# First modulation in four parts, keys and values growing in PSUM across them

## The chip, the cores and the metric

The kernel runs on one core of a Trainium2 chip. The core has five engines with a queue each: TensorE (PE in the profile, with its weight loads as PEld), VectorE (DVE), ScalarE (ACT), GpSimd (POOL) and SyncE (SP), which here issues the loads and stores. Matrix products read SBUF and add up in PSUM, which has eight banks of 512 f32 columns by 128 partitions. The metric is the device time in microseconds (us); lower is better.

## The reference

Two layers of a diffusion backbone over 512 latent tokens and 256 context tokens, width 1024. Layer 0 is windowed grouped-query attention (16 query heads of 64, 4 key and value heads, a sink logit, QK-norm, 2-D rotary positions), layer 1 is bidirectional retention; each is followed by a SwiGLU. Everything is modulated by six vectors made from a condition `c` (or `c_ctx`). What matters here is the beginning of layer 0:

```python
mx = jnp.split(c_act @ ada_w[i] + ada_b[i], 6, axis=-1)
mc = jnp.split(cc_act @ ada_w[i] + ada_b[i], 6, axis=-1)
h_x = modulate(rms_norm(x, norm1_g[i]), mx[0], mx[1])
h_c = modulate(rms_norm(y_ctx, norm1_g[i]), mc[0], mc[1])
...
q_x, k_x, v_x = jnp.split(h_x @ w_qkv, [qd, qd + kvd], axis=-1)
q_x = rope_2d(rms_norm(q_x.reshape(B, S, N_HEADS, HEAD_DIM), q_gain), tables)
k_x = rope_2d(rms_norm(k_x.reshape(B, S, N_KV_HEADS, HEAD_DIM), k_gain), tables)
v_x = v_x.reshape(B, S, N_KV_HEADS, HEAD_DIM)
k_c, v_c = jnp.split(h_c @ w_qkv[:, qd:], 2, axis=-1)
k_c = rms_norm(k_c.reshape(B, L, N_KV_HEADS, HEAD_DIM), k_gain)
```

`modulate(h, shift, scale)` is `h * (1 + scale) + shift`; `mx[0]` and `mx[1]` are the shift and the scale of the first normalization, parts 0 and 1 below.

## The kernel before

Activations lie transposed: the 1024 features are eight tiles `k` of 128 partitions, the tokens are columns (stream `s` = 0 has 512 latents, `s` = 1 has 256 context tokens). Each operand of a projection is kept as a rounded high part and a low part that holds the rest, and a product is three matrix products (`mm3`, L138 to L140: high by high, low by high, high by low). Weights arrive as chunks of 128x1024 f32 through `next_w` (L123 loads, ACT casts the high part at L130, DVE subtracts for the low part at L131) in one stream in a fixed order: two key chunks, two value chunks, queries 0, 1 and so on.

The start of layer 0 runs in this order:

- `ada_unit` (L322) makes 512 columns of one modulation part for both conditions: sixteen products, with a stationary operand of two columns, over four loaded tiles of 512 KB, then `ada_finish` copies the two rows (L306), transposes them (L309) and adds the bias (L313). Four units make parts 0 and 1: units 2 and 0 for feature tiles 0 to 3, then units 3 and 1 for tiles 4 to 7. `fold_gain` (L114) folds the gain into the scale.
- `add_square` (L189 to L192) squares on ACT and adds up on DVE; `rms` (L199) sums over partitions with a matrix of ones on PE; `neg_half_rstd` makes the factor from a logarithm, an exponential and a Newton step (L102, L178 to L180).
- `modulate` does three operations for a feature tile: DVE scales (L211), ACT adds the shift and rounds to the high part (L214), DVE makes the low part (L215). The four feature tiles of a half and stream are traced in a row, latents first, then the context.
- When the features are there, `qk_tile` projects a key chunk for latents and then for the context (L138 to L140 into `pj`), and `head_norm` normalizes it: squares, a block matrix of ones `bd` on PE (L391), the factor, and for latents the rotation (a shuffle on DVE L395, a multiplication on POOL L396, a multiplication and an addition on DVE L397 and L398). Then four copies and differences for a pair of heads write the split keys (L425 to L429).
- Six value tiles of 128 tokens follow, each with 24 products of 256 columns into a bank of `pT` (L442 to L444) and a copy by DVE (L446).
- `make_q(j)` projects a pair of query heads for latents and context, takes the sums of squares per token (L468), rotates (L471 to L474) and splits (L480 to L483). `make_q(0)` and `make_q(1)` come ahead of the attention blocks, the others between them.
- `attend` handles a block of 128 queries of one key head: scores (L534 into `S2`), mask and minimum (L535), exponential (L102), normalization (POOL, L548), transposes on PE (L557), products with the values (L569). Three more modulation units are made between blocks by `ada_unit_late` (L336), which uses four groups of 32 columns of the array with a stationary operand padded to 32 columns.

No part of this start has an order written out: the framework's planner takes the instructions in traced order as priorities and orders each engine by its own estimate of what is ready. A tile with a tag shares a number of buffers; an instruction that needs one waits until the earlier owner's last reader is done.

Of the kernel before, what the change touches and what calls it, by code (L numbers as in the profile page):

```python
# [8 lines left out]
F32 = mybir.dt.float32  # L9
# [16 lines left out]
RH = 4  # L26
# [26 lines left out]
def dit_kernel(ctx, tc, xT, cT, crow, small, consts, masks, tabs0, tabs1, jtab, adaN, adaT, wst, out):  # L53
# [212 lines left out]
    St = ExitStack()  # L266
    st_p = St.enter_context(tc.tile_pool(name="st", bufs=1, reuse_waits="tile"))
    nc.sync.dma_start(cst, consts)
    ccol = cp.tile([P, 8, 2], F32, name="ccol")
    rows_t = cp.tile([P, 512], F32, name="rows")  # L270
    silu(ccol, sm_t[:, C_C:C_C + 16].rearrange("p (k s) -> p k s", s=2))
# [3 lines left out]
    dec = sm_t[:, C_DEC:C_DEC + 8]  # L275
    lg = cp.tile([P, 8], F32, name="lg")
    t1 = cp.tile([P, 8], F32, name="lg_t1")
    t2 = cp.tile([P, 8], F32, name="lg_t2")
    t3 = cp.tile([P, 8], F32, name="lg_t3")
    nc.scalar.activation(t1, dec, AF.Abs)  # L280
    lnexp(t1, t1, AF.Exp, scale=-1.0)
    nc.vector.tensor_scalar(t2, t1, 2.0, None, op0=add)
    nc.vector.reciprocal(t2, t2)
    nc.vector.tensor_tensor(t1, t1, t2, op=mult)
    nc.vector.tensor_tensor(t2, t1, t1, op=mult)
    NTERM = 10
    nc.vector.tensor_scalar(t3, t2, 1.0 / (2 * NTERM + 1), None, op0=mult)
    for k in range(NTERM - 1, 0, -1):
        nc.vector.scalar_tensor_tensor(t3, t3, 1.0 / (2 * k + 1), t2, add, mult)
    nc.vector.scalar_tensor_tensor(t3, t3, 1.0, t1, add, mult)  # L290
    nc.vector.tensor_scalar(t1, dec, 0.0, None, op0=ALU.min)
    nc.vector.scalar_tensor_tensor(lg, t3, -2.0, t1, mult, add)
    dcol = cp.tile([P, 4, RH], F32, name="dcol")
    nc.vector.tensor_scalar(dcol[:, 0, :], lg[:, 0:4], 128.0, None, op0=mult)
    nc.vector.tensor_scalar(dcol[:, 1, :], lg[:, 4:8], 640.0, None, op0=mult)
    nc.vector.tensor_scalar(dcol[:, 2, :], lg[:, 4:8], 384.0, None, op0=mult)
    nc.vector.tensor_scalar(dcol[:, 3, :], lg[:, 4:8], -1.0, None, op0=mult)

    ccol32 = cp.tile([P, 8, 32], F32, name="ccol32")
    nc.gpsimd.memset(ccol32, 0.0)  # L300
    nc.gpsimd.tensor_copy(ccol32[:, :, 0:2], ccol)

    def ada_finish(u, o, m):

        part, d0 = u // 2, u % 2 * 4
        nc.scalar.copy(rows_t[0:m, :], o[0:m, :])  # L306
        t = pO()
        for i in range(4):
            nc.tensor.transpose(t[:, m * i:m * i + m], rows_t[0:m, i * P:(i + 1) * P], ident[0:m, 0:m])  # L309
        tv = t[:, 0:4 * m].rearrange("p (d s) -> p d s", s=m)  # L310
        for s in range(2):
            col = mods[0, s][:, part, d0:d0 + 4]
            nc.vector.tensor_tensor(col, tv[:, :, s], sm_t[:, C_ADAB + 4 * u:C_ADAB + 4 * u + 4], op=add)  # L313

    def ada_unit(u, pool, tag, bufs):

        o = pj()
        for kk in range(4):
            w = T(pool, 1024, tag, bufs)
            nc.sync.dma_start(w, adaN[u, kk])  # L320
            for a in range(2):
                nc.tensor.matmul(o[0:2, :], ccol[:, 2 * kk + a, :], w[:, a * 512:(a + 1) * 512],  # L322
                                 start=kk + a == 0, stop=kk + a == 4)
        ada_finish(u, o, 2)

    def ada_unit_late(u):

        part, d0 = u // 2, u % 2 * 4
# [122 lines left out]
    def make_q(j):  # L451
# [5 lines left out]
        for s in range(2):  # L457
# [6 lines left out]
            if s == 0:  # L464
                tot = pj(12)
# [617 lines left out]
```

## Time and profile before

| | us |
|---|---|
| median of 3 runs | 1861.93 (1860.24 to 1863.08) |
| profiled execution, its time | 1867.23 |
| its span | 1865.4 |
| first key product on PE starts | 40.40 |
| last product of query 1 starts | 112.23 |

Rows of the order of work give the start, the duration, the engine, the line, the operation with output and inputs, and in brackets the idle time before it and what ended it. A PE duration includes the depth of the pipeline, so the pace of a run of products is the distance between starts. A group row gives total busy time, mean duration in ns and the idle time of the engine just before. A row of stretches gives length, busy time (and instructions) of PE, PEld, DVE, ACT and POOL, the granted PE clock, the DMA share and GB/s.

### The profile page before, as it was taken

Reading aid. Unit: us, or ns where it says so; the run is one execution under the profiler, and the core shown is the slowest. Engines: PE = TensorE matmul, PEld = TensorE weight load, DVE = VectorE, ACT = ScalarE, POOL = GpSimd, SP = SyncE. Lnnn points to the kernel's source line nnn. Section 1 sums busy time; section 2 is a strip of 40 time slices with the busy share of each in tenths; the row PEclk is TensorE's granted clock in tenths of the full one; section 3 lists DMA queues with packets and bytes.
Section 4 is the critical chain, followed back from the end, with each engine's and each line's share of the span. In section 5 each row is a group of like instructions: output and inputs, shape, how many; then the busy total and the mean of one; then the engine's idle time right before and its main releaser. Section 6 shows DMA issues by size and latency. Waiting matters only on the chain.

```text
span 1865.4 us, 24307 instructions
## 1 busy us (share of the span) xinstructions
PE 1823.1 (98%) x9787; PEld 1513.8 (81%) x9787; DVE 1036.7 (56%) x1806; ACT 628.5 (34%) x1067; POOL 151.2 (8%) x247
## 2 busy tenths in 40 slices
PE   8899999999999999999999999999999999999999
PEld 2777776778888888888878888888888888888887
DVE  6677786888554545363675543552643664443433
ACT  5556675543221212121252322422322442222221
POOL 0034333410000000000011000010010000000000
PEclk9999999999999999999999999999999999999999
DMA  8110006534332325162521220220321223323232
GB/s 303 60 36 24 13 30 198 197 119 147 102 102 91 114 78 168 53 219 69 170 69 46 68 90 23 91 70 21 102 80 34 68 91 102 97 95 101 92 102 79
DMA packets 50945, 177.97 MB, mean 95 GB/s; under 512 B 5648, under 2 KB 6032, under 8 KB 50576
## 3 DMA queue, kind: packets, MB, share of 16 engines
q1 hardware_dynamic: 50832, 176.41, 29.2%
q8 instruction: 77, 1.26, 0.3%
q14 instruction: 36, 0.29, 0.0%
HBM read 174.29 MB, written 2.10 MB: 95 GB/s over the span
## 4 chain that ended last, share of the span: by engine, by line
PE 84%; DVE 7%; ACT 3%; DMA 2%; issue 2%; POOL 1%; SPq 0%; ACTq 0%; DVEq 0%; POOLq 0%
PE pj L138 9%; PE pj L139 9%; PE pj L140 9%; PE gu L138 9%; PE gu L139 9%; PE gu L140 9%; PE guc L140 2%; PE guc L139 2%; PE guc L138 2%; PE pv L138 2%; PE pv L140 2%; PE pv L139 2%; PE pv L834 2%; PE pv L835 2%; PE pv L833 2%
## 5 line engine op out<-in xcount | busy, mean ns | idle before, releaser
L130 ACT CAST whi<-wraw 128x1024 fp32r<-128x1024 f32 x216 | 226.2, 1047 | 394.5 <-PE pj L140 202.5
L131 DVE TENSOR_TENSOR wlo<-wraw,whi 128x1024 fp32r<-128x1024 f32 x216 | 270.0, 1250 | 155.0 <-ACT whi L130 154.3
L138 PE MATMUL gu<-h,whi 128*128 128x512 f32 (+1 forms) x736 | 280.1, 382 | 3.0 <-DVE res L918 3.0
L139 PE MATMUL gu<-h,wlo 128*128 128x512 f32 (+1 forms) x736 | 279.8, 381 | 0.0
L140 PE MATMUL gu<-h,whi 128*128 128x512 f32 (+1 forms) x736 | 279.6, 381 | 0.0
L138 PE MATMUL pj<-h,whi 128*128 128x512 f32 (+1 forms) x544 | 197.7, 364 | 2.8 <-DVE res L225 2.4
L139 PE MATMUL pj<-h,wlo 128*128 128x512 f32 (+1 forms) x544 | 193.5, 356 | 0.7 <-DVE wlo L131 0.7
L140 PE MATMUL pj<-h,whi 128*128 128x512 f32 (+1 forms) x544 | 192.8, 355 | 0.0
L225 DVE SCALAR_TENSOR_TENSOR res<-pj,mod,res 128x512 f32<-128x512 f32 (+1 forms) x160 | 104.7, 656 | 127.1 <-PE pj L140 127.1
L138 PEld LDWEIGHTS gu<-h,whi 128*128 128x128 f32 x736 | 139.0, 189 | 28.9 <-ACT h L214 3.6
L140 PEld LDWEIGHTS gu<-h,whi 128*128 128x128 f32 x736 | 139.0, 189 | 26.8 <-DVE h L215 0.4
L139 PEld LDWEIGHTS gu<-h,wlo 128*128 128x128 f32 x736 | 138.9, 189 | 25.3
L248 DVE CUSTOM_DVE_ANT_0 junk<-adaw,crow_sb,small_sb 128x1024 bf16<-128x1024 f32 x100 | 134.6, 1346 | 34.8 <-DMA adaw<-in_adaT_dram 33.3
L138 PE MATMUL pj<-ax,whi 128*128 128x512 f32 x352 | 138.2, 393 | 0.0
L139 PE MATMUL pj<-ax,wlo 128*128 128x512 f32 x352 | 137.3, 390 | 0.0
L140 PE MATMUL pj<-ax,whi 128*128 128x512 f32 x352 | 136.9, 389 | 0.0
L107 ACT ACTIVATE hn<-gu 128x512 f32<-128x512 f32 x44 | 26.3, 597 | 285.0 <-PE gu L140 285.0
L138 PEld LDWEIGHTS pj<-h,whi 128*128 128x128 f32 x544 | 105.3, 194 | 17.8 <-DVE res L225 3.3
L139 PEld LDWEIGHTS pj<-h,wlo 128*128 128x128 f32 x544 | 105.3, 194 | 14.0 <-issue 1.5
L140 PEld LDWEIGHTS pj<-h,whi 128*128 128x128 f32 x544 | 105.3, 194 | 12.0
L676 DVE TENSOR_TENSOR hn<-hn,gu 128x512 f32<-128x512 f32 x44 | 30.2, 687 | 134.7 <-ACT hn L107 134.7
L140 PE MATMUL guc<-h,whi 128*128 128x256 f32 x352 | 99.6, 283 | 0.0
(232 smaller groups left out, 3398.4 us busy)
## 6 DMA issues: line engine op xcount, KB each, us to landing
wraw<-in_wst_dram SPq DMA_DIRECT2D x216, 512.0 KB, 3.5
adaw<-in_adaT_dram SPq DMA_DIRECT2D x68, 512.0 KB, 3.7
adan<-in_adaN_dram SPq DMA_DIRECT2D x16, 512.0 KB, 7.8
wraw<-in_adaN_dram SPq DMA_DIRECT2D x12, 512.0 KB, 4.1
res<-in_xT_dram SPq DMA_DIRECT2D x16, 256.0 KB, 6.0
res<-in_cT_dram SPq DMA_DIRECT2D x8, 256.0 KB, 7.1
crow_sb<-in_crow_dram SPq DMA_DIRECT2D x2, 1024.0 KB, 5.0
out_dram<-res SPq DMA_DIRECT2D x8, 256.0 KB, 2.0
```

The costliest lines, as they stand in the source:

```text
L107: ins = nc.scalar.activation(out_, in_, AF.Silu)
L130: nc.scalar.copy(hi, raw)
L131: nc.vector.tensor_tensor(lo, raw, hi, op=sub)
L138: nc.tensor.matmul(o, whi, xhi, start=first, stop=False)
L139: nc.tensor.matmul(o, wlo, xhi, start=False, stop=False)
L140: nc.tensor.matmul(o, whi, xlo, start=False, stop=last)
L225: nc.vector.scalar_tensor_tensor(res[d], o, mods[l, s][:, part, d:d + 1], res[d], mult, add)
L248: after(nc.vector.tensor_tensor_reduce(junk, w, row, 1.0, bias, mult, add, col), behind)
L676: nc.vector.tensor_tensor(t, t, uo, op=mult)
L833: nc.tensor.matmul(vo, hi[:, tok], wk_[0][:, cs], start=k == 0, stop=False)
L834: nc.tensor.matmul(vo, hi[:, tok], wk_[1][:, cs], start=False, stop=False)
L835: nc.tensor.matmul(vo, lo[:, tok], wk_[0][:, cs], start=False, stop=k == KT - 1)
```

## The change

1. *Modulation in quarters.* `adaQ` holds the weights of parts 0 and 1 so that one `ada_quarter` of four loaded tiles makes shift and scale of two feature tiles for both conditions. It uses 32-column groups as the late units do: 32 products of 128 columns, one copy, two transposes, six small DVE operations with the gain folded in. The four units of before go; the three late ones stay (`ada_unit`, with the padded stationary operand `ccol`).
2. *An order written out.* The loads are traced in a fixed sequence: latents, quarter 0, three weight chunks, quarter 1, context, the fourth chunk, quarters 2 and 3, rotary tables, masks. PE, DVE and ACT then follow a written order (`manual_schedule`) in which feature tiles are modulated two at a time (`hidden0`: both scalings, both high parts, then both low parts).
3. *Keys and values grow in PSUM.* `keys(s, q)` and `values(s, q)` add the products of the two feature tiles of quarter `q`. Both latent key chunks, the context keys and three banks with two value tiles each stay open over the whole section: all eight banks with the two of `pT`.
4. *After it*, PE alone has a written order: the remaining latent values, the key sums, the pieces of query 0 (`make_q` now returns four pieces) between them, and the last values. All key rotation is on DVE (`rope_key`), the context's two key chunks are normalized as one 512-column tile, and the values are copied by ACT. The score banks open after these copies.
5. The chain that computes the retention decay (`lg`, `dcol`) moves from the start to just ahead of the attention blocks.

```diff
@@ the modulation of the first normalization
-    def ada_unit(u, pool, tag, bufs):
-
-        o = pj()
-        for kk in range(4):
-            w = T(pool, 1024, tag, bufs)
-            nc.sync.dma_start(w, adaN[u, kk])
-            for a in range(2):
-                nc.tensor.matmul(o[0:2, :], ccol[:, 2 * kk + a, :], w[:, a * 512:(a + 1) * 512],
-                                 start=kk + a == 0, stop=kk + a == 4)
-        ada_finish(u, o, 2)
...
+    def ada_quarter_load(q):
+        w = []
+        for i in range(4):
+            w.append(T(st_p, 1024, "adan", 8))
+            nc.sync.dma_start(w[i], adaQ[q, i // 2, i % 2])
+        return w
+
+    def ada_quarter(q, w):
+
+        o = pT()[:, 0:256]
+        for part in range(2):
+            for k2 in range(4):
+                for j in range(4):
+                    k = 2 * k2 + j // 2
+                    c0 = (k % 4) * 256 + j % 2 * P
+                    nc.tensor.matmul(o[32 * j:32 * j + 32, part * P:(part + 1) * P], ccol[:, k, :],
+                                     w[2 * part + k // 4][:, c0:c0 + P], start=k2 == 0, stop=k2 == 3)
+        rows = T(cp, 256, "rows", 2)
+        nc.scalar.copy(rows, o)
+        t = pT()[:, 0:256]
+        for part in range(2):
+            nc.tensor.transpose(t[:, part * P:(part + 1) * P], rows[:, part * P:(part + 1) * P], ident)
...
+        for s in range(2):
+            col = mods[0, s][:, 0:2, 2 * q:2 * q + 2]
+            nc.vector.tensor_tensor(col, tv[:, s, 0], bias, op=add)
+            nc.vector.tensor_tensor(col, tv[:, s, 1], col, op=add)
+            fold_gain(0, s, 0, 2 * q, 2 * q + 2)
...
-    for c in range(2):
-        if c == 0:
-            for s, res in ((0, xr), (1, cres)):
-                for k in range(KT):
-                    add_square(s, k, res[k], eng=nc.vector, tmp=(t_sq, t_sc)[s])
-                rms(s, bank=pT)
-        else:
-            ada_unit(3, st_p, "adan", 8)
-            ada_unit(1, st_p, "adan", 8)
-        for s, res in ((0, xr), (1, cres)):
-            fold_gain(0, s, 0, 4 * c, 4 * c + 4)
-            for d in range(4 * c, 4 * c + 4):
-                h[s].append(h_tiles(s))
-                modulate(0, s, 0, d, res, h[s][d], tmp=t_st)
...
+    res0 = [load_stream(0), None]
+    wq = [ada_quarter_load(0)]
+    load_w(rp, "wraw", 2)
+    load_w(rp, "wraw", 2)
+    load_w(st_p, "adan", 8)
+    wq.append(ada_quarter_load(1))
+    res0[1] = load_stream(1)
+    load_w(st_p, "adan", 8)
+    wq += [ada_quarter_load(2), ada_quarter_load(3)]
...
+    kvx = [pj(), pj()]
+    kvc = pO()
+    kvv = [T(ps_v, 512, "kvv", 3) for _ in range(3)]
...
+    def hidden0(s, *ks):
+        y, ts = ssq[s], []
+        for k in ks:
+            h[s].append(h_tiles(s))
+            ts.append(T(st_p, 512, "hs", 3)[:, :NTOK[s]])
+            nc.vector.scalar_tensor_tensor(ts[-1], res0[s][k], acol[0, s, 0][:, k:k + 1], y, mult, mult)
+            nc.scalar.activation(h[s][k][0], ts[-1], AF.Identity, bias=mods[0, s][:, 0, k:k + 1])
+        for k, t in zip(ks, ts):
+            nc.vector.scalar_tensor_tensor(h[s][k][1], t, mods[0, s][:, 0, k:k + 1], h[s][k][0], add, sub)
+
+    def keys(s, q):
+        for j in range(2):
+            o = kvx[j] if s == 0 else kvc[:, j * SC:(j + 1) * SC]
+            for k in (2 * q, 2 * q + 1):
+                ws = slice(k * P, (k + 1) * P)
+                (whi, wlo), (xhi, xlo) = wkv[j], h[s][k]
+                for i, (a, b) in enumerate(((whi, xhi), (wlo, xhi), (whi, xlo))):
+                    nc.tensor.matmul(o, a[:, ws], b, start=k + i == 0 and (s == 0 or j == 0),
+                                     stop=k == KT - 1 and i == 2, skip_group_check=s == 1)
...
+    with tc.manual_schedule(engines={mybir.EngineType.PE, mybir.EngineType.DVE, mybir.EngineType.Activation}):
+        stats0(0)
+        split_w(st_p)
+        ada_quarter(0, wq[0])
+        hidden0(0, 0, 1)
+        split_w(st_p)
+        keys(0, 0)
+        split_w(rp)
+        squares0(1)
+        ada_quarter(1, wq[1])
+        hidden0(0, 2, 3)
+        values(0, 0)
+        rms(1, bank=pT)
+        keys(0, 1)
+        ada_quarter(2, wq[2])
+        hidden0(1, 0, 1)
+        hidden0(1, 2, 3)
+        hidden0(0, 4, 5)
+        split_w(rp)
+        values(0, 1)
+        ada_quarter(3, wq[3])
+        hidden0(1, 4, 5)
+        keys(1, 0)
+        keys(1, 1)
+        hidden0(0, 6, 7)
+        keys(0, 2)
+        hidden0(1, 6, 7)
+        values(1, 0)
+        values(1, 1)
+        for i, mt in enumerate(mtmp):
+            nc.vector.tensor_copy(mask[:, 4 * i * P:4 * i * P + mt.shape[1]], mt)
+        keys(1, 2)
+        keys(0, 3)
+        keys(1, 3)
...
-            nc.gpsimd.tensor_tensor(qn, qn, rope0[:, 0:512], op=mult)
...
+    for a, b, o in zip(kn, ksq, (kvx[0], kvc, kvx[1])):
+        nc.scalar.activation(b, o, AF.Square)
+        nc.scalar.activation(a, o, AF.Identity, scale=qk_gain[:, 1:2])
...
+        nc.vector.stream_shuffle(yy, t, swap16)
+        nc.vector.tensor_tensor(t, t, rope0[:, 0:512], op=mult)
+        nc.vector.tensor_tensor(yy, yy, rope0[:, 512:1024], op=mult)
+        nc.vector.tensor_tensor(t, t, yy, op=add)
...
+    with tc.manual_schedule(engines={mybir.EngineType.PE}):
+        values(0, 2)
+        rope_key(kn[0])
+        key_factor(0)
+        q0[0]()
+        key_factor(1)
+        for e in range(2):
+            kx[e] = key_parts(e, kn[0])
+        q0[1]()
+        for e in range(2):
+            k1, k2 = key_parts(e, kn[1])
+            kc[e], kc[2 + e] = ((k1[:, c], k2[:, c]) for c in HALVES)
+        q0[2]()
+        values(0, 3)
+        q0[3]()
+        values(1, 2)
+        values(1, 3)
+    vt = []
+    for t in range(6):
+        v = T(akv, 256, "v", 6)
+        nc.scalar.copy(v, kvv[t // 2][:, t % 2 * 256:t % 2 * 256 + 256])
+        vt.append(v)
+    psS.close()
```

More of the change, by code (lines that the diff above doesn't have):

```diff
@@ L52, in dit_kernel @@
 @with_exitstack
[L53 removed]
+def dit_kernel(ctx, tc, xT, cT, crow, small, consts, masks, tabs0, tabs1, jtab, adaQ, adaN, adaT, wst, out):
     nc = tc.nc
@@ L295, in dit_kernel @@
[L295 to L313, printed above, removed]
```

258 lines of the change are left out of this document (136 added, 122 removed).

## The prediction

> **What bounds the kernel now.** I read the page first, then the busy time by stretches, then the order of work on PE around the start, then the groups and single rows that carry durations. The page:
>
> ```profile
> span 1865.4 us, 24307 instructions
> PE 1823.1 (98%) x9787; PEld 1513.8 (81%) x9787; DVE 1036.7 (56%) x1806; ACT 628.5 (34%) x1067; POOL 151.2 (8%) x247
> ```
>
> PE bounds the span. The change touches the start alone, so I cut that out: busy time before the first key product, from there to the end of the second query projection, and the attention blocks.
>
> ```profile
> 0.00:40.40 40.40, 32.81 (x81) 6.79 (x81) 24.96 (x73) 20.77 (x39) 0.86 (x7) 1.00 0.86 329
> 40.40:112.40 72.00, 62.76 (x377) 54.34 (x376) 48.94 (x92) 37.99 (x71) 7.99 (x8) 0.95 0.21 66
> 112.40:300.00 187.60, 182.30 (x1360) 141.48 (x1360) 148.05 (x467) 122.99 (x295) 74.18 (x166) 1.00 0.14 47
> ```
>
> Columns: length, busy PE, PEld, DVE, ACT, POOL, granted clock, DMA share, GB/s. Attention keeps PE busy 97% and DVE 79%, with little DMA: whatever is saved ahead of it moves it forward whole. In the first 40.4 us PE looks busy, but with this:
>
> ```profile
> L322 PE MATMUL pj<-adan,ccol 128*2 128x512 f32 x64 | 30.3, 626 | 6.7 <-DMA adan<-in_adaN_dram 6.7
> 6.29 9.01 PE L322 MATMUL pj<-adan,ccol 128*2 128x512 f32 x16 [6.29 <-DMA adan<-in_adaN_dram]
> 16.75 7.03 PE L322 MATMUL pj<-adan,ccol 128*2 128x512 f32 x16 [0.38 <-DMA adan<-in_adaN_dram]
> 40.40 0.50 PE L138 MATMUL pj<-h,whi 128*128 128x512 f32 x1
> 99.97 0.87 PE L534 MATMUL S<-k,q 128*128 128x256 f32 x6
> 107.07 0.41 PE L534 MATMUL S<-k,q 128*128 128x256 f32 x2
> 112.23 0.28 PE L140 MATMUL pj<-h,whi 128*128 128x256 f32 x1
> ```
>
> Four modulation units of 7 us with two useful output rows. The first key product starts at 40.40, the last query-1 product ends at about 112.4; less eight score products in between (1.3), **111.1** is the mark to compare with: keys, values, queries 0 and 1 projected.
>
> **The change, walked through.** Its first section fixes the order on PE, DVE and ACT, so it can be followed engine by engine with the durations of before; all times of the new kernel are estimates so worked out. Transfers:
>
> ```profile
> 0.00:4.00 4.00, 0.00 (x0) 0.00 (x0) 0.38 (x4) 2.53 (x3) 0.86 (x7) 1.00 0.47 90
> 4.00:10.00 6.00, 3.71 (x5) 0.63 (x6) 3.26 (x21) 0.68 (x3) 0.00 (x0) 1.00 1.00 403
> 10.00:20.00 10.00, 8.95 (x24) 1.85 (x23) 5.19 (x11) 5.41 (x9) 0.00 (x0) 1.00 1.04 399
> 10.73 0.63 ACT L189 ACTIVATE y<-res 128x512 f32<-128x512 f32 x1 [6.02 <-DMA res<-in_xT_dram]
> ```
>
> 0.36 MB by 4 us, then 0.4 MB a us; the first latent tile, 2.6 MB into the queue, landed at 10.73 where the count reaches it at about 9.6, so a landing lags by some 1.2. New order: constants, latents (2.1 MB), quarter 0 (2.1), three projection weights (1.6), quarter 1, context (1.0), fourth weight, quarters 2 and 3. Landings: latents 10.1, quarter 0 15.4, weights 16.7/18.0/19.3, quarter 1 24.5, context 27.1, quarter 2 33.5, quarter 3 about 40. Eight staging tiles serve these 18 loads, so on SP the last tile of quarter 1 waits for PE's first products, and the context, the fourth weight and all later loads queue behind it; there are 2.9 MB already in flight then, so the queue does not run dry. Compute rows:
>
> ```profile
> 23.71 1.13 PE L199 MATMUL pT<-y,ones_sb 128*128 128x512 f32 x2
> 51.12 1.97 PE L391 MATMUL pj<-sq,const_sb 128*128 128x512 f32 x2 [0.58 <-ACT sq L390]
> 28.73 1.41 DVE L211 SCALAR_TENSOR_TENSOR hs<-res,acol,y 128x512 f32<-128x512 f32 x2
> 43.39 1.41 DVE L215 SCALAR_TENSOR_TENSOR h<-hs,mod,h 128x512 fp32r<-128x512 f32 x2
> 36.28 0.88 DVE L211 SCALAR_TENSOR_TENSOR hs<-res,acol,y 128x256 f32<-128x256 f32 x2
> 42.26 1.22 DVE L131 TENSOR_TENSOR wlo<-wraw,whi 128x1024 fp32r<-128x1024 f32 x1
> 41.04 1.04 ACT L130 CAST whi<-wraw 128x1024 fp32r<-128x1024 f32 x1
> 294.69 0.64 PE L336 MATMUL pj<-wraw,ccol 128*32 128x128 f32 x16
> 295.26 0.44 PE L557 MATMUL pT<-const_sb,pr 128*128 128x128 f32 x2
> 296.02 0.31 PE L341 MATMUL pj<-const_sb,rows 128*128 128x128 f32 x1
> 40.56 0.57 ACT L306 COPY rows<-pj 2x512 f32<-2x512 f32 x1 [1.92 <-PE pj L322]
> 42.12 0.23 DVE L313 TENSOR_TENSOR mod<-pO,small_sb 128x4 f32<-128x4 f32 x2
> ```
>
> A quarter uses the form of the late units: 16 instructions issue in 0.57 us, and a quarter has 64, so 2.3 us of PE, then a copy (at most 0.57), two transposes (0.5), six small DVE operations (1.0). Four quarters take 11 us of PE with their transposes where four units took 30; that is the part removed. From the ones product to the modulating DVE operation takes 5.0 us (23.71 to 28.73); with the product at 1.97, as it is after an idle PE, 5.9.
>
> - Latents squared by 11.5, factor at 17.3. Quarter 0: products end 17.6. Its copy stands on ACT behind the cast of the first weight, which waits for that landing (16.7): 18.2; columns on DVE, behind the weight's 1.22 us, at 20.0.
> - First pair: 1.41 + 1.41 on DVE; its first high part lets PE start keys at **21.5**, against 40.40. Second and third weight follow on DVE to 25.6.
> - The context's squares wait for 27.1 and hold ACT to 27.9; behind them stands quarter 1's copy, whose products end at 28.3 anyway. Its columns at 30.2, pair done 33.1.
> - Quarter 2 stands on PE behind four value tiles, the context's ones product and keys: products 35.9 to 38.2, columns 40.1. DVE then does two context pairs (4 × 0.88) and a latent pair (2.8) to 46.8, and the fourth weight's split to 48.1.
> - Quarter 3's products end at 44.3, but its copy is behind the split on ACT: 47.3, columns 49.1. DVE: context pair 1.8, latent 2.8, context 1.8, masks 0.8: 56.6.
>
> From 47.8, after quarter 3's transposes, I find no PE instruction whose inputs come later than its turn. What is left on PE, by these intervals:
>
> ```profile
> 43.77 0.39 PE L139 MATMUL pj<-h,wlo 128*128 128x512 f32 x1
> 44.00 0.40 PE L140 MATMUL pj<-h,whi 128*128 128x512 f32 x1
> 53.10 0.42 PE L139 MATMUL pj<-h,wlo 128*128 128x256 f32 x1
> 53.32 0.42 PE L140 MATMUL pj<-h,whi 128*128 128x256 f32 x1
> 54.88 0.28 PE L139 MATMUL pj<-h,wlo 128*128 128x256 f32 x1
> 55.00 0.28 PE L140 MATMUL pj<-h,whi 128*128 128x256 f32 x1
> 108.49 1.05 PE L468 MATMUL pj<-const_sb,sq 128*128 128x2 f32 x8 [1.02 <-ACT sq L463]
> ```
>
> A 512-column product takes 0.23, a 256-column one 0.12 (0.21 in a slow stretch). Left: context keys 48 × 0.12 = 5.8; latent keys 24 × 0.23 = 5.6; values 96 × 0.12 = 11.5; two queries 48 × 0.23 + 48 × 0.12 = 17; three key sums 3; query sums 2 × 1.4. In all 45.7, so query 1 ends at **93.5** where before it was 111.1: **-17.6**.
>
> **Additions.** The stretch at half speed at 53 shows that a PE gap (47.8 to 50.0) is followed by about 3.4 us at half clock; PE now waits from 44.3 to 47.8, so I add 1.7. The decay chain, 21 small DVE operations, moves from the idle start to the attention's start:
>
> ```profile
> 5.80 1.77 DVE L289 SCALAR_TENSOR_TENSOR lg_t<-lg_t,lg_t 128x8 f32<-128x8 f32 x9
> 60.55 0.68 DVE L397 TENSOR_TENSOR y<-y,rope 128x512 f32<-128x512 f32 x1
> L396 POOL TENSOR_TENSOR hn<-hn,rope 128x512 f32<-128x512 f32 x2 | 3.4, 1697 | 69.3 <-DVE y L395 69.3
> L428 DVE TENSOR_TENSOR k<-hn,k 64x512 fp32r<-64x512 f32 x4 | 2.8, 688 | 0.5 <-ACT k L426 0.3
> ```
>
> At 0.2 each that is 4 us of DVE, which costs between 0 (PE bounds) and 4 (DVE bounds); I take 1, near the lower end, since DVE stands idle a fifth of the attention. Key rotary on DVE: two multiplications of 0.68 replace two of 1.7 on POOL; shorter per key, covered by the values and query 0 on PE, nothing. The value copies go to ACT and the score banks come free only after them, at about 84; until 93.5 PE has query 1 to do, nothing. Sum: -17.6 + 1.7 + 1.0 = **-15**. The profiled execution took 1867.23 (span 1865.4), 5.3 above the median 1861.93; the same 15 off the median gives **1847**.
>
> [...] The first unit above took 9.01 for 16 products and the second 7.03; the products at 53.10, after the gap, are spaced 0.21 against 0.12 at 54.88, and the granted clock of that whole stretch is 0.95: 3.6 us lost in 72, about 7 us at half speed. So the rows charge a gap with one slow stretch. [...]
>
> **Rivals.**
> 1. *The last quarter waits for a staging tile.* If its last load gets the tile of the fourth weight, it is issued after the split at 48.1 and lands 3.5 later, about 52:
>
> ```profile
> wraw<-in_wst_dram SPq DMA_DIRECT2D x216, 512.0 KB, 3.5
> ```
>
>    Columns at 54.5, everything after +5.4, and another slow stretch 1.7: **1854**. Against it: quarter 2's tiles come free at 36.
> 2. *DVE bounds the new second half.* From 56.6 to 93.5 it has three keys (2 × 2.8 rotary, 3 × 2.1 factors, 12 × 0.69 splits: 20), two queries of 5.5 (weight 1.22, rotary 2.1, splits 2.2) and the decay chain of 4: 35 us in 37. At the 79% that DVE held beside a full PE this takes 44: +7, **1854**. For it: 35 in 37 leaves no room for a wait. Against it: the third key (7.7) is not due until later heads.
> 3. *Half clock through the first section.* PE's work from 21.5 to 62 is 35 us at full clock; all of it at half ends near 91, not 62: +29, **1876**, slower than before. It decides from nine slow stretches (9 × 1.7 us = 15). Against it: the 0.95 of before, with 9 us of idle PE in its 72.
> 4. *The round trips eat it.* Each quarter crosses PE, ACT, PE, DVE in fixed order; the walk has columns at 20.0, 30.2, 40.1, 49.1. If each trip is 3.7 longer, the change does not do what it says and nothing is gained: **1862**. Against it: each handover above is counted with the row of the operation itself and the queue ahead of it.
>
> **Numbers.** Forecast 0.60 (own range 1841 to 1853: without the two additions and with DVE 3 us ahead, or with both doubled and one late pair), rival 1 0.11, rival 2 0.14, rival 3 0.08, rival 4 0.07. Leaving out rival 3 and half of 4 and the forecast's far tail gives 1840 to 1860. A measurement here tells about 0.2% (3.7 us) from no change: faster 0.82, same 0.08, slower 0.10.
>
> **What would show it.** Right: first key product near 21.5, four modulation groups of about 2.5 us on PE, end of query 1 near 94 to 96, attention as before and 15 us earlier. Wrong: PE idle beyond 50 us before quarter 3 (rival 1), PE waiting on DVE between 62 and 100 (2), granted clock under 0.8 from 20 to 60 (3), columns much more than 10 us apart (4), or an attention stage longer than before because its order is planned anew.

## The result and the profile after

| | us | ratio to before (95%) |
|---|---|---|
| before, median of 5 runs beside it | 1861.93 (1860.24 to 1866.28) | |
| after, median of 5 runs | 1853.34 (1851.35 to 1854.41) | 0.9951 (0.9936 to 0.9966) |

The change makes the kernel 8.6 us faster; 15 were forecast. The profiled execution of after took 1854.34. Its page:

```profile
span 1852.5 us, 24666 instructions
PE 1798.5 (97%) x9969; PEld 1517.3 (82%) x9969; DVE 1032.3 (56%) x1808; ACT 629.2 (34%) x1064; POOL 150.1 (8%) x243
```

PE still bounds. It is 24.6 us less busy than in the profile of before that was shown, 20.7 less than in a second one (before_again, below), and only part of that came out as time. PE's order of work in the new section (start, duration, what was waited for):

```profile
12.49 2.04 PE L199 MATMUL pT<-y,ones_sb 128*128 128x512 f32 x2 [12.49 <-DVE lg_t L705]
14.47 3.59 PE L310 MATMUL pT<-adan,ccol 128*32 128x128 f32 x64
18.56 0.44 PE L316 MATMUL pT<-const_sb,rows 128*128 128x128 f32 x2 [0.50 <-ACT rows L313]
21.57 0.80 PE L390 MATMUL pj<-h,whi 128*128 128x512 f32 x1 [2.57 <-ACT h L379]
...
29.34 0.44 PE L316 MATMUL pT<-const_sb,rows 128*128 128x128 f32 x2 [1.44 <-ACT rows L313]
...
35.77 1.95 PE L310 MATMUL pT<-adan,ccol 128*32 128x128 f32 x64
38.22 0.44 PE L316 MATMUL pT<-const_sb,rows 128*128 128x128 f32 x2 [0.49 <-ACT rows L313]
...
41.46 1.96 PE L310 MATMUL pT<-adan,ccol 128*32 128x128 f32 x64
46.50 0.39 PE L401 MATMUL kvv<-whi,h 128*128 128x256 f32 x1 [3.09 <-ACT whi L147]
46.77 0.44 PE L316 MATMUL pT<-const_sb,rows 128*128 128x128 f32 x2
...
91.22 0.28 PE L140 MATMUL pj<-h,whi 128*128 128x256 f32 x1
...
94.25 0.61 PE L521 MATMUL pj<-const_sb,sq 128*128 128x2 f32 x4
```

The four quarters are there, the first key product starts at 21.57, and the longest PE gap behind it is at 43.4 to 46.5. Query 1's last product starts at 91.22, and its last sums of squares end at 94.9.

To see where the gain went, the trace is cut at three marks that both kernels have: the start of query 1's last sum of squares, of the last value product of the attention, and of the first product of the feed-forward. The profiled executions differ among themselves, so a second one of before (before_again) stands beside the one shown earlier. Stretches of before, whose first row runs to the first mark (columns as in the prediction):

```profile
0.00:114.00 114.00, 97.07 (x466) 62.23 (x466) 75.47 (x164) 60.31 (x114) 9.93 (x15) 0.97 0.44 158
114.00:336.10 222.10, 214.61 (x1595) 163.30 (x1594) 166.64 (x531) 142.62 (x344) 84.76 (x194) 0.98 0.20 65
336.10:402.80 66.70, 63.92 (x363) 56.02 (x360) 59.67 (x80) 28.68 (x43) 23.35 (x14) 0.97 0.47 156
```

The same of before_again, and what follows the third mark:

```profile
0.00:111.70 111.70, 96.06 (x465) 61.26 (x466) 74.70 (x164) 60.32 (x114) 9.97 (x15) 0.98 0.45 162
111.70:329.60 217.90, 211.79 (x1595) 161.65 (x1594) 166.82 (x531) 142.60 (x344) 84.98 (x194) 1.00 0.20 66
329.60:396.40 66.80, 64.03 (x364) 56.08 (x361) 59.78 (x80) 28.79 (x43) 22.77 (x14) 0.97 0.47 157
396.40:1858.80 1462.40, 1447.39 (x7372) 1232.26 (x7370) 734.81 (x1033) 397.35 (x568) 33.06 (x25) 1.00 0.30 92
```

And the four of after:

```profile
0.00:94.60 94.60, 72.58 (x641) 61.84 (x642) 68.31 (x154) 54.06 (x100) 4.75 (x9) 0.98 0.51 191
94.60:317.10 222.50, 211.79 (x1599) 163.61 (x1598) 168.49 (x543) 149.33 (x355) 91.67 (x196) 0.99 0.18 58
317.10:389.10 72.00, 65.52 (x365) 57.38 (x362) 60.65 (x80) 27.65 (x42) 20.56 (x14) 0.95 0.47 165
389.10:1852.50 1463.40, 1448.64 (x7372) 1234.42 (x7371) 734.87 (x1033) 398.21 (x569) 33.12 (x25) 1.00 0.30 92
```

- **Front:** 111.7 to 94.6, 17.1 gained (19.4 against the other profile of before).
- **Attention:** PE is busy 211.79 in before_again and 211.79 in after, but the stretch grows from 217.9 to 222.5: PE's idle time, length less busy, goes from 6.1 to 10.7. 4.6 given back. The first profile of before is as long as after (222.1) for another reason: granted clock 0.98, idle 7.5.
- **Stage between attention and feed-forward** (output projection, gated addition, modulation): 66.8 to 72.0, 5.2 given back, though nothing in it was edited. PE's idle time there goes from 2.8 to 6.5; the other 1.5 is longer busy time, at a granted clock of 0.95 against 0.97.
- **The rest:** +1.0.

Sum -6.3 between these two profiles, which bracket with the other pair (-12.9) the -8.6 of the medians.

### The profile page after: what moved, and what is told of

Its sections match the earlier page's. It is cut to its first block, busy times and chain, and to the rows that moved or that the text cites. A ratio compares the mean times of both kernels' runs of the same rounds, so it can differ in the third digit from the quotient of the medians.

```text
span 1852.5 us, 24666 instructions
## 1 busy us (share of the span) xinstructions
PE 1798.5 (97%) x9969; PEld 1517.3 (82%) x9969; DVE 1032.3 (56%) x1808; ACT 629.2 (34%) x1064; POOL 150.1 (8%) x243
## 4 chain that ended last, share of the span: by engine, by line
PE 86%; DVE 6%; ACT 3%; DMA 2%; POOL 2%; issue 2%; SPq 0%; DVEq 0%; ACTq 0%; POOLq 0%
PE pj L138 9%; PE pj L139 9%; PE pj L140 9%; PE gu L138 9%; PE gu L139 9%; PE gu L140 9%; PE guc L140 2%; PE guc L139 2%; PE guc L138 2%; PE pT L635 2%; PE pv L138 2%; PE pv L140 2%; PE pv L139 2%; PE pv L943 2%; PE pv L944 2%; PE pv L942 2%
## 5 line engine op out<-in xcount | busy, mean ns | idle before, releaser
L130 ACT CAST whi<-wraw 128x1024 fp32r<-128x1024 f32 x212 | 222.2, 1048 | 387.8 <-PE pj L140 200.5
L131 DVE TENSOR_TENSOR wlo<-wraw,whi 128x1024 fp32r<-128x1024 f32 x212 | 264.7, 1248 | 153.3 <-ACT whi L130 152.5
L138 PE MATMUL pj<-h,whi 128*128 128x512 f32 (+1 forms) x512 | 185.3, 362 | 6.9 <-DVE res L225 6.1
L139 PE MATMUL pj<-h,wlo 128*128 128x512 f32 (+1 forms) x512 | 182.1, 356 | 1.0 <-DVE wlo L131 1.0
L140 PE MATMUL pj<-h,whi 128*128 128x512 f32 (+1 forms) x512 | 181.9, 356 | 0.0
L225 DVE SCALAR_TENSOR_TENSOR res<-pj,mod,res 128x512 f32<-128x512 f32 (+1 forms) x160 | 104.7, 656 | 128.7 <-PE pj L140 128.6
L248 DVE CUSTOM_DVE_ANT_0 junk<-adaw,crow_sb,small_sb 128x1024 bf16<-128x1024 f32 x100 | 134.9, 1349 | 36.7 <-DMA adaw<-in_adaT_dram 32.9
L138 PEld LDWEIGHTS pj<-h,whi 128*128 128x128 f32 x512 | 98.7, 193 | 21.0 <-DVE res L225 7.2
L139 PEld LDWEIGHTS pj<-h,wlo 128*128 128x128 f32 x512 | 98.6, 193 | 13.0 <-DVE wlo L131 1.4
L140 PEld LDWEIGHTS pj<-h,whi 128*128 128x128 f32 x512 | 98.6, 193 | 12.1 <-issue 0.4
```

The lines of the kernel that those rows point to most:

```text
L130: nc.scalar.copy(hi, raw)
L131: nc.vector.tensor_tensor(lo, raw, hi, op=sub)
L138: nc.tensor.matmul(o, whi, xhi, start=first, stop=False)
L139: nc.tensor.matmul(o, wlo, xhi, start=False, stop=False)
L140: nc.tensor.matmul(o, whi, xlo, start=False, stop=last)
L225: nc.vector.scalar_tensor_tensor(res[d], o, mods[l, s][:, part, d:d + 1], res[d], mult, add)
```

## The experiments

The experiments ran in three groups. The runs of a group share a chip and the runs of before beside them, and the ratios are against those.

### Where the missing gain went: the condition rows

The modulation sums of the middle stage need `crow_sb`, a load of condition rows into a tile of the pool `wo`, which is opened after the attention and takes memory that the attention's tiles held. The SP queue's waits, in before_again:

```profile
SPq L230 <- DVE stat L541: 9.7, 1, 9.7
```

and in after:

```profile
SPq L230 <- PE pO L647: 15.7, 1, 15.7
```

The order of work of after at that place:

```profile
316.25 0.75 DVE L225 SCALAR_TENSOR_TENSOR res<-pj,mod,res 128x512 f32<-128x512 f32 x1
...
317.54 0.33 SPq L230 DMA_DIRECT2D crow_sb<-in_crow_dram  x1
...
323.67 1.28 ACT L107 ACT_TABLE_LOAD   x1 [3.79 <-DMA crow_sb<-in_crow_dram]
...
326.06 1.28 DVE L248 CUSTOM_DVE_ANT_0 junk<-adaw,crow_sb,small_sb 128x1024 bf16<-128x1024 f32 x1 [2.36 <-ACT crow_sb L107]
```

The load now waits for the last value products and is issued 1.3 us after the first gated addition (316.25); in before_again it is issued at 324.11, 4.5 ahead of it (328.65). ACT then idles 3.79 for the landing and DVE 2.36 for ACT. The first modulation sum starts 9.8 after the first gated addition, 7.0 in before_again. The theory was that this late load makes the stage longer; the rival, that the order of the work does. Two runs move the load. **rows_early** (from after) lets query 0's weight tile take the first place in the attention's pool, so that `wo` overlays tiles that come free sooner:

```diff
+    wsel[0] = 2
+    w_q0 = next_w(ap, 1)
...
-    wsel[0] = 2
-    q0 = make_q(0)
+    q0 = make_q(0, w_q0)
```

> The changed kernel with the pool of the attention laid out so that its two weight tiles come first (the split of query 0's weights is traced ahead of the normalized keys); the condition rows of the output projection, which take the same memory once the attention pool is closed, then lie on tiles that are read for the last time by the last query projection. Theory 1 (the 6 us that are lost between the end of the attention and the first FFN group come from these rows: their load waits for the last value product and DVE's modulation sums start late): the load is issued at least 5 us ahead of the first gated addition instead of 1 us behind it, PE's 6 us of idle time in that stage shrink to about 2, and the time is 1847 to 1848. Theory 2 (the loss lies in how the planner orders DVE in that stage, whatever the load does): the load moves and the time stays at 1852 to 1854.

**rows_late** (from before) holds the load behind a value product of the last attention block:

```diff
-        nc.sync.dma_start(cr, crow.broadcast_to([P, 2048]))
+        ins = nc.sync.dma_start(cr, crow.broadcast_to([P, 2048]))
+        if late is not None:
+            tc.add_manual_dep(ins.ins, late.ins.name, run_dep, reason="condition rows behind the attention")
...
-    cr = cond_rows(wo_p)
+    cr = cond_rows(wo_p, last_pv[0])
```

> The kernel before with one added wait: the load of the condition rows of the output projection waits for the first value product of the last attention block of the trace. Theory 1: the stage loses 5 to 6 us, 1867 to 1868. Theory 2: the load is late and the time stays at 1862 within 2.

The two kernels themselves ran again on the same chip:

> The changed kernel once more, on the same chip as the two others. Both theories: 1853 within 2, the end of the attention at 317 within 1.5 us of the span, and the first FFN group's end some 6 us later than the attention's gain would give.

> The kernel before once more, for its trace. If the 12.9 us between the two profiled spans are 8.6 in the medians because the first profiled execution of before was a long one, this span is 1859 to 1863, and the stage that is shorter than in the first trace shows where the difference lay. If the span is 1865 again, a profiled execution is longer than a timed one.

Measured: rows_early 1865.19, ratio 1.0019 (1.0010 to 1.0029); rows_late 1861.06, 0.9996 (0.9988 to 1.0005); changed_again 1854.99, 0.9960 (0.9948 to 0.9972); before_again 1860.62 in one run. In changed_again the front ends at 96.9, the attention takes 223.1 and the stage 70.0: the two losses repeat. The stage and, above it, the attention in rows_early:

```profile
94.90:327.70 232.80, 217.82 (x1598) 167.29 (x1599) 168.83 (x541) 146.83 (x351) 89.57 (x197) 0.98 0.19 60
327.70:396.40 68.70, 64.21 (x365) 56.35 (x362) 60.77 (x80) 27.83 (x42) 20.91 (x14) 0.98 0.45 157
```

The stage in rows_late:

```profile
331.00:397.40 66.40, 62.76 (x363) 54.59 (x360) 59.72 (x80) 28.67 (x43) 23.70 (x14) 1.00 0.53 180
```

In rows_late the load is issued at 331.44, 1.3 us behind the first gated addition (330.10), as in after, and the stage is no longer: 66.4 against 66.8, the kernel the same. The lengths hide a little, because this stage ran at a granted clock of 1.00 and that of before_again at 0.97: PE's idle time is 3.6 instead of 2.8. So the late load alone does not make the stage long; that theory falls as the whole cause. But the run repeats the late load and not the late sums. The first sum starts 7.8 behind the first gated addition, against 7.0 in before_again and 9.8 in after, since ACT loads its table here before the rows land, at 333.80, and in after only behind them, at 323.67:

```profile
333.80 1.28 ACT L107 ACT_TABLE_LOAD   x1
```

rows_early shortens the stage by 1.3 (against changed_again) to 3.3 (against after), which leaves 1.9 of the 3.2 to 5.2 us. This rest goes with the order on DVE. PE's waits for the gated addition in the stage (total, times, longest), in before and in after:

```profile
PE pj L138 <- DVE res L225: 2.4, 2, 2.0
PE pj L138 <- DVE res L225: 6.1, 2, 4.3
```

In rows_early this wait is 4.1. DVE's order of work around the third gated addition (L225) and the third modulation sum (L248), in before_again:

```profile
341.00 0.74 DVE L225 SCALAR_TENSOR_TENSOR res<-pj,mod,res 128x512 f32<-128x512 f32 x1
341.66 2.77 DVE L248 CUSTOM_DVE_ANT_0 junk<-adaw,crow_sb,small_sb 128x1024 bf16<-128x1024 f32 x1
```

and in changed_again:

```profile
333.36 3.42 DVE L248 CUSTOM_DVE_ANT_0 junk<-adaw,crow_sb,small_sb 128x1024 bf16<-128x1024 f32 x1
336.70 0.74 DVE L225 SCALAR_TENSOR_TENSOR res<-pj,mod,res 128x512 f32<-128x512 f32 x1
```

The sum comes first in all nine traces with the change, rows_early among them, and the addition first in all five without it. The third addition starts 12.4 us behind the first in before_again, 13.2 in rows_late, 16.1 in rows_early, 17.5 in changed_again and 18.5 in after. So both the load and DVE's new order delay it, the order more; no run set that order alone.

And rows_early loses the whole gain elsewhere: with a front as early as after's (94.9) its attention takes 232.8 instead of 222.5. Idle PE there is 15.0 (232.80 less 217.82), and the same products keep PE busy 217.82 instead of 211.79 at a granted clock of 0.98 (0.99 in after). Its edit touches no attention instruction. What changed is the order that the planner gave them. Read by the names of output and inputs, PE's products in the attention stand in one sequence in before_again, rows_late and the two runs with other units below, in a second one in after, changed_again and every run from after below but query_last; rows_early and query_last have each a sequence of their own.

### What makes the gain

Four parts of the change, one at a time. The prediction wrote the gain as one walk; the question was whether it comes from the cheaper modulation products, from the projection products that run between them, or from the written order, and whether the gap at 43.4 costs anything.

**units_by_groups** (from before): the four units use the 32-column groups of the late ones; nothing else changes.

```diff
-    def ada_unit(u, pool, tag, bufs):
...
-    def ada_unit_late(u):
+    def ada_unit_late(u, pool=rp, tag="wraw", bufs=2, bank=pj):
...
+            ada_unit_late(3, st_p, "adan", 8, pO)
+            ada_unit_late(1, st_p, "adan", 8, pO)
```

> The kernel before with its four first units in the form of the late ones (four groups of 32 columns, 2.3 us of products instead of 7), nothing else changed. Theory A (the gain of the start comes from projecting the first features while the later ones are still being made, and the PE time of the units hardly counts, since the loads end at 36 us and DVE's modulation at 49): first key product at 35 to 38 instead of 40.2, time 1858 to 1860. Theory B (the 19 us of removed PE time are the gain): first key product near 22 to 25, time near 1846.

**products_after** (from after): all key and value products of the first section stand behind the modulation on PE.

```diff
         split_w(st_p)
-        keys(0, 0)
         split_w(rp)
...
         hidden0(0, 2, 3)
-        values(0, 0)
         rms(1, bank=pT)
-        keys(0, 1)
         ada_quarter(2, wq[2])
...
+        keys(0, 0)
+        values(0, 0)
+        keys(0, 1)
+        values(0, 1)
         keys(1, 0)
```

> The changed kernel with all key and value products of the first section moved behind the last modulated feature in the written order (same products, same order among them, the quarters and the pairs as they are). Theory A: PE has 25 us of products left at about 46 instead of 15, so the section ends near 71 instead of 61, and 9 to 10 us of the gain are gone: 1862 to 1865. Theory B: the products only move within the section, 1854 to 1856.

**planner_order** (from after): the first section's order is left to the planner.

```diff
-    with tc.manual_schedule(engines={mybir.EngineType.PE, mybir.EngineType.DVE, mybir.EngineType.Activation}):
+    if True:
```

> The changed kernel without the written order of its first section: the planner orders PE, DVE and ACT there from the same traced instructions. Theory C (the written order carries part of the gain): the first section ends 3 us or more later than 61 and the time is 1857 or more. Theory D (what counts is only that the products can start early): end of the section within 2 us, time 1852 to 1857, the spread that another order of the attention brings.

**split_later** (from after): the fourth weight is split behind quarter 3's modulation, so that quarter 3's copy does not stand behind it on ACT.

```diff
         hidden0(0, 4, 5)
-        split_w(rp)
         values(0, 1)
         ada_quarter(3, wq[3])
         hidden0(1, 4, 5)
+        split_w(rp)
```

> The changed kernel with the fourth weight split after quarter 3 and the third context pair instead of ahead of quarter 3's copy; its values are not needed before the last two quarters. By the walk of the prediction quarter 3's columns come 1.0 to 1.2 us earlier and PE's gap of 3 us before 46.5 shrinks by as much: 1 us gained at the end of the section, time 1852 to 1854. If PE stands behind the split itself, the gap stays.

Measured: units_by_groups 1866.62, ratio 1.0032 (1.0021 to 1.0044); products_after 1864.96, 1.0019 (1.0007 to 1.0031); planner_order 1857.94, 0.9983 (0.9973 to 0.9992); split_later 1854.08, 0.9964 (0.9948 to 0.9979).

products_after has the same cheap quarters, but PE has nothing beside them until they are done. Its stretches:

```profile
20.00:40.00 20.00, 12.23 (x198) 7.62 (x198) 16.63 (x43) 10.94 (x22) 0.00 (x0) 0.66 1.03 416
40.00:60.00 20.00, 15.59 (x91) 14.09 (x92) 12.34 (x28) 6.35 (x12) 0.00 (x0) 0.83 0.14 54
```

Query 1's mark comes at 105.6, 11.0 later than in after and 8.7 later than in changed_again, and the kernel's whole gain is gone. Part of this is the clock: 0.66 and 0.83 over 40 us, 0.96 in after from 21.57 to 61.00. Stage by stage not all of the front is lost, though: 105.6 is still 6.1 ahead of before_again's 111.7. So the early products carry 8.7 to 11.0 of the 14.8 to 17.1, the rest of the change the other 6.1, and the total has nothing left because the attention (223.8) and the stage (70.9) are as long as with the change. units_by_groups takes the other side. PE's order of work there, and ACT's row for the key weight:

```profile
37.98 0.33 PE L318 MATMUL pO<-const_sb,rows 128*128 128x128 f32 x1 [1.85 <-ACT rows L316]
43.59 0.80 PE L138 MATMUL pj<-h,whi 128*128 128x512 f32 x1 [5.28 <-ACT whi L130]
...
42.51 1.03 ACT L130 CAST whi<-wraw 128x1024 fp32r<-128x1024 f32 x1
```

The units need little PE time, but the first key product comes at 43.59 instead of 40.40: PE waits 5.28 for the cast of the key weight, which ACT does at 42.51, behind three feature tiles of the modulation, and in before at 37.61. So taking PE time off the units alone gains nothing here; ACT's other order and the lower clock (0.90 to the mark) are part of this result. Most of the front's gain is that projection products run in the idle time between the quarters. Whether they would have found that time beside the wide units, with their 30 us of PE, no run shows. The written order is worth some 3 to 4.6 us of the time (planner_order against changed_again 1854.99 and after 1853.34), 1.4 to 3.7 of it at the front, whose mark comes at 98.3. In split_later the gap ahead of quarter 3's transposes is 2.42, waiting for the copy, where after has 3.09, and the time is that of after. The edit shortens the gap by 0.7 us only, so it does not tell what the gap costs.

### The clock, the place of query 0, and the rotary engine

The slower units_by_groups could be explained by the clock alone. **units_groups_warm** adds six products without use to each unit (from units_by_groups), **gaps_filled** ten such products to the new start (from after):

```diff
+        t = bank()
+        if tag == "adan":
+            for _ in range(6):
+                nc.tensor.matmul(t, ones, w[:, 0:512], start=True, stop=True)
+        t = t[:, 0:P]
```

> The kernel before with its first units in column groups, as in units_by_groups, and six products of the ones matrix with a loaded weight tile added to each unit, whose results nobody reads; they give PE back the busy time that the wide units had. Theory E (units_by_groups is 4 to 5 us slower than the kernel before because PE, less busy, runs at half clock for 24 us of the start): the half-clock stretches between 20 and 60 shrink to one of 3.4 us or none, first key product at 40 or earlier, time 1859 to 1862. Theory F (it is slower through another order of DVE and ACT): stretches shrink and the time stays at 1865 to 1867.

```diff
+        t = pT()
+        for _ in range((0, 1, 0, 3)[q]):
+            nc.tensor.matmul(t, ones, res0[0][0], start=True, stop=True)
+        t = t[:, 0:256]
...
+        squares0(0)
+        spare = pT()
+        for k in range(4):
+            nc.tensor.matmul(spare, ones, res0[0][k], start=True, stop=True)
+        rms(0, bank=pT)
...
```

> The changed kernel with ten products of the ones matrix and a latent tile added where PE waits in the first section (four ahead of the latents' sums, two behind quarter 0's transposes, one and three ahead of the transposes of quarters 1 and 3), whose results nobody reads. Theory E (half clock costs the new start 2 to 4 us): no half-clock stretch between 20 and 60, the first keys end by 25 instead of 26, the query-1 sums by 93 to 94 instead of 94.6 to 96.9, time 1850 to 1852. Against it: the added products delay what waits behind them, time 1854 or more.

**query_last** (from after) puts query 0's pieces behind the last values in PE's written order, **rotary_pool** (from after) gives one multiplication of the key rotation back to POOL:

```diff
         key_factor(0)
-        q0[0]()
         key_factor(1)
+        values(0, 3)
...
         values(1, 2)
         values(1, 3)
+        for piece in q0:
+            piece()
```

> The changed kernel with all of query 0's products behind the last values in PE's written order. By the prediction the place of query 0 only covers the keys' factors: PE would wait for nothing else, since values stand in its place, and the query-1 sums come at 95 to 97 as before; but query 0's shaping on ACT and DVE (2.7 and 4.3 us) comes 9 us later and the first score cannot start before it. If the first score waits, the time is 1856 to 1860; if query 1's products cover it, 1853 to 1856.

```diff
-        nc.vector.tensor_tensor(t, t, rope0[:, 0:512], op=mult)
+        nc.gpsimd.tensor_tensor(t, t, rope0[:, 0:512], op=mult)
```

> The changed kernel with the first multiplication of the key rotary back on GpSimd (1.7 us instead of 0.68 for each of two tiles). The prediction counted this at nothing: 1853 to 1856. If DVE bounds the stretch from 57 to 94, it is faster, by up to 1.4; if the first score waits for the keys, slower by about 1 us.

Measured: units_groups_warm 1867.88, ratio 1.0028 (1.0017 to 1.0038); gaps_filled 1855.74, 0.9959 (0.9945 to 0.9972); query_last 1863.49, 1.0009 (0.9998 to 1.0019); rotary_pool 1854.62, 0.9956 (0.9943 to 0.9970).

With the products without use the granted clock up to query 1's mark is 0.94 (to 119.3), in units_by_groups 0.90 (to 116.5), but PE is busy 100.13 up to it instead of 83.78, and the mark comes 2.8 later. Its order of work:

```profile
42.30 5.42 PE L320 MATMUL pO<-adan,ones_sb 128*128 128x512 f32 x12
47.55 0.27 PE L322 MATMUL pO<-const_sb,rows 128*128 128x128 f32 x1
47.58 0.47 PE L138 MATMUL pj<-h,whi 128*128 128x512 f32 x1
```

The last unit with its six products (twelve records) runs to 47.55 and the first key follows at once, so the run cannot say what a free clock would have been worth to that kernel; this stays open. In after, filling the gap (PE is busy from 44.53 to 47.4 in it) leaves the time as it was (1855.74 against 1853.34) and the granted clock up to the mark too, 0.98 in both: the clock of the new start, 0.96 over the section, is no loss that such products mended.

query_last was meant to measure query 0's place. But its mark for query 1 comes at 95.3, after's at 94.6 and 96.9: the place costs nothing at the front. The 8.5 to 10 us are lost later. The stretch of its attention:

```profile
95.30:329.20 233.90, 220.14 (x1599) 168.73 (x1599) 169.41 (x542) 147.39 (x352) 88.50 (x196) 0.96 0.17 55
```

Idle time is 13.8 (233.90 less 220.14) against 10.7, and the products that took PE 211.79 now take 220.14 at a granted clock of 0.96 (0.99 in after). As in rows_early, an edit ahead of the attention made the planner order the attention in another way; the gaps grew, and the clock was lower. rotary_pool is after within its interval: no difference shows between the engines for that multiplication.

### The attention: more waits for the normalization

PE's waits from 100 to 320 us in after (total, times, longest):

```profile
PE pT L635 <- POOL pr L626: 6.5, 13, 1.1
PE pj L284 <- DMA wraw<-in_adaN_dram: 1.7, 1, 1.7
```

and in before_again:

```profile
PE pT L557 <- POOL pr L548: 2.9, 9, 0.5
...
PE pj L336 <- DMA wraw<-in_adaN_dram: 0.7, 1, 0.7
```

The transposes wait 6.5 instead of 2.9 for POOL's normalization, a late modulation unit 1.7 instead of 0.7 for its load. These two rows grow by 3.6 and 1.0, as much as the idle time did (4.6). The attention takes 221.2 to 223.8 in all runs that keep the change and have after's order of products (products_after, planner_order, split_later, gaps_filled, rotary_pool too), and 217.5 to 219.2 in those without it (before_again, rows_late, both units runs), but for the first profile of before with its lower clock. So the loss belongs to the change and not to chance, nor to the first section's order. Which of its parts makes the planner order the attention in this way was not told apart. Nor is the order the only difference: behind the mark after still has the third key's factor and split to do, some 4.3 us on ACT, which before has done by then, and whether the waits come from this work or from the order stays open. No run fixed the attention's order by hand, which would be the test, and no version measured is clearly faster than after.

## Why the prediction came out as it did

The time, 1853.34, lies in the range of 1840 to 1860 and the sign was right; the size was not: 8.6 for 15. It is just above the forecast's own 1841 to 1853 and beside 1854, the price of rivals 1 and 2, so only the traces tell these apart. The width of the range took in 8.4 to 9.8 us of losses that the sum did not have; in that part the number is luck.

- **Front, -17.6 + 1.7: right.** Measured -17.1 (after) and -14.8 (changed_again) against before_again, -19.4 and -17.1 against the profile that the walk was read from. (The two ends of the walk are not quite the same place: its 93.5 counts query 1's sums of squares, its 111.1 stops ahead of the last of them.) First key 21.57 for 21.5; quarter 3's products at 41.46, ended at 43.4 for 44.3; its transposes at 46.77, done 47.2 for 47.8; masks last, done at 55.8 for 56.6 by the row of DVE's order below. The slow stretch of 1.7 is there, but in another place: in after at the first keys alone, whose starts are 0.43 apart up to 24.7 (granted clock 0.50 from 21.3) and 0.23 from there, while behind the gap products of 256 columns go at 0.12 (granted clock 1.00 from 43.4 to 56). In changed_again the granted clock up to the mark is 0.95 (0.98 in after), and its front is 2.3 longer.

That row of after:

```profile
55.14 0.69 DVE L434 CAST mask<-hn 128x512 bf16<-128x512 f32 x2
```

- **The gap at quarter 3: right in place and cause.** The written reason was the copy behind the fourth weight's split; in the trace a value product stands there too and waits 3.09 for the same cast. What it costs stays open: split_later shortens it by 0.7 us only, and gaps_filled fills it with products without use and starts the transposes 1.2 later.
- **"The part removed", 11 us of PE for 30: counted right, but not what gains by itself.** units_by_groups removes most of it and is slower by 5. Most of the front's gain is that products fill the time between (products_after loses 8.7 to 11.0 of it).
- **Decay chain, +1.0: wrong place.** The planner put it back into the start: its first steps run on DVE between the latents' sums of squares, its nine L705 steps right behind them from 12.27, so nothing is added at the attention.
- **Value copies, score banks, key rotary, nothing each: right** as far as runs show: rotary_pool is the same, and the first mark came in time.
- **"Attention as before and 15 us earlier": this step failed.** It set everything behind query 1 at nothing but the decay chain's 1.0. The attention gave back 4.6 to 5.2 and the stage behind it 3.2 to 5.2. The last case of the list of what would make it wrong, an attention planned anew, is what happened, and it was given no term in the sum. The stage behind the attention was on no list. A load's place there hangs on which tiles of the attention its memory overlays, which accounts for at most 3.3 of it; the rest goes with DVE's new order there, in which the third gated addition stands behind one more modulation sum.
- **Rival 3, half clock through the first section, did not occur.** The granted clock from 21.57 to 61.00 is 0.96, with PE busy 34.41 of 39.43. That a whole section could run at half clock was the author's assumption: up to 120 us the trace of before has two slow stretches, of 3.4 us each, from 51.3 and from 95.6. In products_after the clock is 0.66 from 20 to 40, with PE busy 12.23 of the 20. What sets it was not shown.
- **Rivals 1, 2 and 4 did not occur.** No quarter waited for a load; PE is idle 1.4 from 61 to 96:

```profile
21.57:61.00 39.43, 34.41 (x368) 30.31 (x369) 28.86 (x65) 18.80 (x35) 0.00 (x0) 0.96 0.60 228
61.00:96.00 35.00, 33.57 (x216) 29.11 (x215) 27.93 (x47) 24.68 (x50) 4.34 (x4) 1.00 0.14 47
```

  and the transposes at 18.56, 29.34, 38.22 and 46.77 are 8.6 to 10.8 apart, as walked.

## What to carry to other kernels

Here a written order could be walked row by row to a microsecond; what the planner ordered behind it was not foreseen, so a gain ahead of a planned stage deserves a term for that stage's new order (here 4.6 to 5.2 us in the attention and 3.2 to 5.2 in the stage behind it, and some 10 more after two edits that touched no instruction of the attention). Making the modulation cheaper gained nothing by itself: most of the front's gain came when later products were put into the idle time. And an experiment that moves one thing ahead of a planned stage must be read stage by stage, since its total may speak of the planner alone.

## What the runs showed of the hardware

- A kernel with less work was slower: units_by_groups keeps PE busy 83.78 to its mark instead of 97.07, and its granted clock there is 0.90 instead of 0.97. Its order on ACT differs too, so the clock's share is not told apart.
- The granted clock can read full where products are slow: in after it is 1.00 from 14.4 to 18.1, and quarter 0's 64 products take 3.59 there; those of quarters 2 and 3 take 1.95 and 1.96.
- A slow stretch can be longer than the gap ahead of it, and a gap can have none behind it: in after PE waits 2.57 ahead of 21.57, and the granted clock is 0.50 for 3.4 us, from 21.3 to 24.7; it waits 3.09 ahead of 46.50, and the clock is 1.00 from 43.4 to 56. In query_last PE's longest waits in the attention were these (total, times, longest)

```profile
PE pT L633 <- POOL pr L624: 7.6, 11, 1.3
PE pj L284 <- DMA wraw<-in_adaN_dram: 2.2, 2, 1.8
```

  yet the granted clock is 0.96 over 233.9 us, and PE was busy 8.4 us longer than in after for the same number of products. That the gaps cause it is not shown.
- The same program does not meet the same stretches each time: the attention of before ran at 0.98 in one profiled execution and at 1.00 in the other, 222.1 against 217.9 us. Of these 4.2 us, 2.8 are PE's busy time for the same products. A difference of 4 us between two single traces can come without any change of the kernel.
